# Attention outputs kept in DRAM as high and low part, and layer 1's turns in another place

## The chip, the cores and the metric

The kernel runs on one core of a Trainium2 chip. The metric is device time in microseconds (us): the median of three runs of the whole program. The engines are TensorE (PE), VectorE (DVE), ScalarE (ACT), GpSimd (POOL) and SyncE (SP); each takes its instructions from its own queue in order, and they wait for each other by semaphores.

## What is computed

Two layers of a diffusion trunk on 512 latent tokens and 256 context tokens of width 1024. Layer 0 mixes tokens by differential attention (8 heads, each with two 64-wide maps), layer 1 by neighbourhood attention on an 8 x 64 grid (16 heads of 64, taken two at a time as 8 groups). Each is followed by an output projection and a squared-ReLU MLP. Cut to what matters:

```python
for i in range(2):
    h_l = modulate(rms_norm(x, norm1_g[i]), mod_l[0], mod_l[1])      # h_c likewise, from ctx
    y = mixer_i(h_l, h_c)                   # attention, then @ w_o
    x = x + mod_l[2] * y_l
    x = x + mod_l[5] * squared_relu_mlp(modulate(rms_norm(x, norm2_g[i]), ...))
    # layer 0 updates ctx in the same way

def diff_attend(q, k, v, lam):              # layer 0
    p = softmax(einsum('bqhmd,bkhmd->bhmqk', q, k) * scale)
    return einsum('bhqk,bkhe->bqhe', p[:, :, 0] - lam * p[:, :, 1], v)
    # then rms_norm per head with gain subln_g, then @ w_o

# layer 1: a query sees an 8 x 16 window of the latent grid, with a relative bias, and all context
# y = softmax(q k + bias) v @ w_o
```

All products are fp32 made of three passes: an operand is kept as a high part (an ACT copy that rounds to the PE's fp32r form) and a low part (the value less the high part, on DVE or POOL), and `PASSES` multiplies high by high, high by low and low by high. A tile of such *parts* is `[128, 2, n]` with the part as its middle index.

## The kernel before

Per layer the kernel runs an attention stage and then its MLP. The attention stage is software-pipelined over heads (layer 0) or groups (layer 1). Inside it PE, SP and POOL issue in the order in which the program is written, and that order is a string of words (`END0`, `CYCLE1` and so on, lines 38 to 53) which `run()` goes through, once per head. DVE and ACT are placed by a scheduler from what depends on what. A word is a kind and a tile number, and a prime sends it to the head before. The kinds:

- `w`, `c`: loads of a weight chunk (SP) and its split in parts (`wsplit`, lines 145 and 146: ACT copies, POOL or, in layer 1, DVE subtracts). In the last string `c` stands for the output projection's weights.
- `Q` i, a or b: half of the QKV projection of token tile i (line 408; twelve matmuls to a half). The second half ends in a norm per head (`qk_normed`, lines 415 to 423), whose result is the tile Y.
- `U`: the *turn*: transposes of q and k of two token tiles (line 499; in layer 1 lines 634 and 636) and their splits into parts (`q_split`, `k_split`, lines 427 to 450).
- `S`: scores and softmax (lines 517 to 529; in layer 1 lines 656 to 670). `T`: probabilities transposed and split (lines 541 to 544; 686 to 688). `V`: weighted sum (line 552; 701), in layer 1 with the output put into a tile T `[128, 512]` by lines 708 and 709.
- `O` (layer 0): the normed output is transposed (line 569), and line 570 copies it on ACT into a tile OT; after every second one line 575 stores 128x256 of it, one value per element, to `oT0` in DRAM. Layer 1's fourth `V` of a group stores 128x512 to `oT1` (line 713).
- `x`: the projection's fetch of a head from `oT0` or `oT1` on SP's queue (line 738), into a staging tile N (layer 1: ST). `X`: the split of that head into parts on ACT (line 743) and then POOL or DVE (line 744), into a tile H or Q.
- `P` i, a or b: the projection of token tile i from three heads each (line 750); `B`: its last weights and gates; `m`, `n`: a chunk of the modulation vectors (lines 257 and 263).

The last head's output does not go through DRAM: `split_last` (lines 782 and 783) splits it into parts where it is made. `END0` and `END1` are the tails of the two attention stages, in which the last head's attention runs beside the projection; what is left of the projection follows in `end()`.

The table of PSUM banks gives tag A two or three banks (projections and turns), B two (T, V and O), S and C the scores and layer 0's turns. Since a bank must be read before it is written again, PE at a `T`, `V` or `O` waits for whoever reads the bank two of them back.

Of the kernel before, what the change touches and what calls it, by code (L numbers as in the profile page):

```python
# [63 lines left out]
class Block:  # L64
# [391 lines left out]
    def head0(self, h, w=None, hT=None, accs=None, split=None):  # L456
# [6 lines left out]
        def tile_(i, acc):  # L463
# [10 lines left out]
            else:  # L474
                t2 = self.sbt('OT' if accs else 'Y', [P, 2, 2, 64])
# [251 lines left out]
    def project(self, l, wo, oT, t0, xsrc, tag_o, tag_h, tag_p, out):  # L727
# [5 lines left out]
        oHL, raws, w0, x0, acc = {}, {}, [], [], {}  # L733
        gate = {}

        def fetch(h):
            st = raws[h] = self.sbt('ST' if 'ST' in self.room else 'N', [P, ntok])
            nc.sync.dma_start(st, oT[h])

        def split(h, eng):  # L740
            st = raws.pop(h)
            u = oHL[h] = self.sbt(tag_o[h // 4], [P, 2, ntok], F32R)
            self.tc.keep_in_program_order(nc.scalar.activation(u[:, 0, :], st, AF.Copy))  # L743
            self.tc.keep_in_program_order(eng.tensor_sub(u[:, 1, :], st, u[:, 0, :].bitcast(F32)))
# [33 lines left out]
        def split_last(st, j):  # L778
            if KT - 1 not in oHL:
                oHL[KT - 1] = self.sbt(tag_o[1], [P, 2, ntok], F32R)  # L780
            u, cc = oHL[KT - 1], slice(256 * j, 256 * j + st.shape[1])
            nc.scalar.activation(u[:, 0, cc], st, AF.Copy)
            nc.vector.tensor_sub(u[:, 1, cc], st, u[:, 0, cc].bitcast(F32))

        def end():
# [147 lines left out]
def hybrid_block(tc, a, out):  # L933
    nc = tc.nc
    with ExitStack() as ctx, ExitStack() as st:
# [9 lines left out]
        with b.psum_phase("ps0", **PS_HEAD0):  # L945
# [184 lines left out]
```

## Time and profile before

| | us |
|---|---|
| median of three runs | 1907.71 (1907.19 to 1908.19) |
| profiled execution | 1907.34 |
| its span on the core | 1905.4 |
| PE busy in it | 1793.9 (94%) |
| DVE, ACT, POOL busy | 1132.7, 829.2, 815.6 |
| mean granted PE clock | 0.979 |

The span is what the profiler saw between the first and the last instruction; 1.9 us of the execution lie around it. Two lines of the profile's page show the course of the span in 40 slices of 47.6 us (a digit is the busy share in tenths, 9 for 90% or more):

```profile
PE   6989999996999999999999998999998989999998
PEclk9999999997999999999999998999999999999999
```

Layer 0's attention takes the first 11 slices and ends in the tenth and eleventh, its MLP goes to the 22nd, layer 1's attention from the 25th to the 32nd, and its MLP is the rest. Stages are told by their stretch in us from the start of the span. In the views below, an operation's line number is that of the kernel before; `PA<-W,Q` names what is written and read by the program's tile names; x12 is a count. A wait is idle time of an engine before an instruction and the instruction that ended it.

### The profile page before, as it was taken

The page shows a single profiled execution, that of the slowest core. Times are in us where ns is not written, and L with a number is a line of the kernel's source. Part 1 is how long each engine was busy: PE and PEld are TensorE (multiplying, and loading weights), DVE is VectorE, ACT ScalarE, POOL GpSimd, SP SyncE. Part 2 cuts the span into 40 slices and gives each one's busy share as a digit, 9 for nine tenths or more (in the row PEclk, how much of TensorE's full clock was granted, in tenths as well). Part 3 has the DMA queues.
Part 4 walks back from the last instruction along what each step waited for, and adds up shares of the span by engine and source line. Part 5 has one row for each costly group of instructions (what it writes and reads, how often), then busy time and mean ns, then how long its engine had stood idle before and what let it go on. Part 6 is the DMA issues. An engine that isn't in the chain of part 4 may idle for free.

```text
span 1905.4 us, 27130 instructions
## 1 busy us (share of the span) xinstructions
PE 1793.9 (94%) x10256; PEld 1570.9 (82%) x10256; DVE 1132.7 (59%) x2158; ACT 829.2 (44%) x1854; POOL 815.6 (43%) x688
## 2 busy tenths in 40 slices
PE   6989999996999999999999998999998989999998
PEld 5878888885789888888888977998898778888886
DVE  4588777785574343343334676778777664444446
ACT  4476767774342212221221245677667342223321
POOL 3655656653224333342442532344335444444443
PEclk9999999997999999999999998999999999999999
DMA  8122222224324343443432132122112323223232
GB/s 327 43 84 78 87 87 87 89 69 159 119 72 140 130 157 111 166 165 112 157 136 73 56 100 64 56 69 84 56 67 89 116 89 99 89 89 107 92 100 77
DMA packets 66499, 197.61 MB, mean 104 GB/s; under 512 B 8192, under 2 KB 23488, under 8 KB 60224
## 3 DMA queue, kind: packets, MB, share of 16 engines
q1 hardware_dynamic: 58608, 186.03, 29.3%
q10 hardware_dynamic: 7760, 9.85, 1.5%
q8 instruction: 80, 1.31, 0.3%
q14 instruction: 51, 0.42, 0.1%
HBM read 180.74 MB, written 15.11 MB: 103 GB/s over the span
## 4 chain that ended last, share of the span: by engine, by line
PE 75%; DVE 11%; ACT 6%; issue 4%; POOL 2%; DMA 2%; ACTq 0%; SPq 0%; POOLq 0%; DVEq 0%
PE PD L830 22%; PE PA L408 14%; PE PA L865 11%; PE PB L865 9%; PE PA L750 4%; PE PA L257 2%; PE PS L517 2%; PE PB L552 2%; PE PB L701 2%; PE PQ L398 1%; PE PS L656 1%; PE PB L686 1%; ACT E L523 1%; PE PB L541 1%; DVE N L311 1%
## 5 line engine op out<-in xcount | busy, mean ns | idle before, releaser
L146 POOL TENSOR_TENSOR W<-R,W 128x1024 fp32r<-128x1024 f32 x142 | 351.3, 2484 | 541.2 <-ACT W L145 541.0
L830 PE MATMUL PD<-Q,W 128*128 128x384 f32 (+2 forms) x1992 | 395.9, 345 | 2.4 <-DVE Q L334 1.1
L830 PEld LDWEIGHTS PD<-Q,W 128*128 128x128 f32 x1992 | 345.7, 188 | 33.7 <-issue 8.6
L145 ACT ACTIVATE W<-R 128x1024 fp32r<-128x1024 f32 (+1 forms) x172 | 172.6, 1021 | 450.5 <-PE PA L865 193.5
L865 PE MATMUL PA<-W,H 128*128 128x512 f32 x1080 | 275.4, 393 | 4.7 <-POOL W L146 3.0
L865 PEld LDWEIGHTS PA<-W,H 128*128 128x128 f32 x1080 | 200.2, 188 | 51.5 <-issue 4.5
L839 DVE TENSOR_TENSOR N<-N 128x768 f32<-128x768 f32 (+1 forms) x64 | 67.0, 1048 | 279.1 <-ACT N L835 170.3
L865 PE MATMUL PB<-W,H 128*128 128x512 f32 x840 | 209.2, 391 | 0.0
L408 PE MATMUL PA<-W,Q 128*128 128x384 f32 (+1 forms) x1008 | 177.4, 331 | 11.2 <-ACT H L446 11.2
L865 PEld LDWEIGHTS PB<-W,H 128*128 128x128 f32 x840 | 157.4, 188 | 33.3
L408 PEld LDWEIGHTS PA<-W,Q 128*128 128x128 f32 x1008 | 163.0, 196 | 12.9 <-ACT H L446 12.9
L296 POOL TENSOR_TENSOR SQ<-SQ,half 128x4 f32<-128x4 f32 (+1 forms) x96 | 99.2, 1034 | 134.0 <-DVE SQ L421 132.9
L842 DVE SCALAR_TENSOR_TENSOR H<-N,H 128x768 fp32r<-128x768 f32 (+1 forms) x64 | 98.1, 1534 | 25.7 <-ACT H L841 25.0
L408 PE MATMUL PA<-WB,H 128*128 128x384 f32 x576 | 108.4, 340 | 0.8 <-DVE Q L469 0.8
L750 PE MATMUL PA<-W,H 128*128 128x512 f32 x384 | 99.1, 409 | 8.0 <-ACT H L743 5.1
L408 PEld LDWEIGHTS PA<-WB,H 128*128 128x128 f32 x576 | 98.6, 188 | 1.8 <-DVE Q L469 1.1
L830 PE MATMUL PD<-H,W 128*128 128x512 f32 (+1 forms) x408 | 94.1, 378 | 2.5 <-DVE SA L290 2.0
L876 DVE TENSOR_TENSOR H<-PA,H 128x512 f32<-128x512 f32 x78 | 53.9, 690 | 69.6 <-PE PA L865 69.6
L750 PEld LDWEIGHTS PA<-W,H 128*128 128x128 f32 x384 | 73.3, 196 | 26.3 <-ACT H L743 5.4
L830 PEld LDWEIGHTS PD<-H,W 128*128 128x128 f32 x408 | 73.8, 188 | 18.0 <-DVE H L334 2.9
L523 ACT ACTIVATE E<-PS,SA 128x768 f32<-128x768 f32 (+1 forms) x96 | 72.8, 759 | 34.6 <-DVE SA L522 31.9
L517 PE MATMUL PS<-Q,Q 128*128 128x256 f32 (+1 forms) x320 | 69.1, 348 | 19.4 <-ACT Q L446 10.3
(210 smaller groups left out, 3056.5 us busy)
## 6 DMA issues: line engine op xcount, KB each, us to landing
R<-in_w_dram SPq DMA_DIRECT2D x128, 512.0 KB
M<-in_wmod_dram SPq DMA_DIRECT2D x48, 1024.0 KB
R<-in_wqa_dram SPq DMA_DIRECT2D x32, 384.0 KB
R<-in_wqb_dram SPq DMA_DIRECT2D x32, 384.0 KB
Y<-in_rpb_dram SPq DMA_DIRECT2D x48, 128.0 KB
bias<-Y SPq DMA_DIRECT2D x48, 128.0 KB
X<-bias SPq DMA_DIRECT2D x8, 768.0 KB
R<-in_woa_dram SPq DMA_DIRECT2D x8, 512.0 KB
```

Of the source, the lines that this page charges most:

```text
L145: high = nc.scalar.activation(w[:, 0, :n], raw, AF.Copy)
L146: low = (eng or nc.gpsimd).tensor_sub(w[:, 1, :n], raw, w[:, 0, :n].bitcast(F32))
L296: nc.gpsimd.tensor_tensor(r, ss, self.half[:, :n], op=ALU.pow)
L408: nc.tensor.matmul(acc[:, :n], hT[kt][:, x, P * i:P * i + P], w[kt // 2][:, y, o:o + n], start=(kt == 0 and p == 0), stop=(kt == KT - 1 an ...
L517: nc.tensor.matmul(s[:, c0:c1], q[:, m, P * i:P * i + P], k[:, m, c0:c1], start=p == 0, stop=p == 1)
L523: nc.scalar.activation(e[:, m, :nk], s, AF.Exp, bias=mx[:, 0:1], accum_out=sm[:, m:m + 1])
L750: nc.tensor.matmul(ps, oHL[h][:, x, c:c + P], w[h // 2][:, y, 512 * (h % 2):512 * (h % 2) + 512], start=(first and h == hs[0] and p == 0), ...
L830: nc.tensor.matmul(ps[:, at:at + b1 - b0], w[kt // 4][:, x, o:o + P], hT[kt][:, y, b0:b1], start=(kt == 0 and p == 0), stop=(kt == KT - 1 ...
L839: nc.vector.tensor_mul(r, r, r)
L842: nc.vector.scalar_tensor_tensor(u[:, 1, :], r, 1.0, u[:, 0, :].bitcast(F32), op0=ALU.mult, op1=ALU.subtract)
L865: nc.tensor.matmul(ps, hd[:, x, P * i - c0:P * i - c0 + P], w[f][:, y, 512 * n:512 * n + 512], start=(f == 0 and p == 0), stop=(f == len(h ...
L876: nc.vector.tensor_add(av, ps, av)
```

## The change

There are four parts.

1. The DRAM tensors `oT0` and `oT1` hold both parts of each output, so that a head is twice the bytes: 768 KB for 384 in layer 0, 512 KB for 256 in layer 1.
2. The parts are made where an output is made. In layer 0's `O`, ACT writes the high part from PSUM and a new DVE operation (128x128, line 571 of the changed kernel) the low part; the store waits for both, and OT has one buffer of twice the size instead of two. In layer 1's fourth `V`, an ACT copy and a DVE subtraction 128x512 go into a new tile OS, which is stored. The last head writes straight into the projection's tile.
3. The projection's fetch goes by DMA straight into its tile of parts, and the words `X` are gone, with their ACT, POOL and DVE instructions and the staging buffers. The fetches stand elsewhere in the tails.
4. In layer 1's strings, V2'' stands right behind T3'', ahead of U4', and U2 right behind Q4b. `END1` is written anew.

The core of the diff:

```diff
-END0 = """x0 x1 x2 x3 S1' O2'' O3'' V4'' T0' U4' n1' X0 V5'' T1' X1 S2' O4'' X2 x4 V0' S3' x5 P0a O5'' T2' X3 P1a
-X4 V1' O0' S4' X5 B0 P0b m0 V2' O1' x6 P1b T3' n0 P2a T4' S5' P2b O2' P3a V3' V4' P3b m1 T5' P4a O3' n1
-X6 P4b V5' P5a P5b O4' O5'"""
-CYCLE1 = """w0 w1 Q0a T3'' U4' Q1a c0 w2 V2'' V3'' Q0b S0' Q1b Q2a S1' Q2b Q3a T0' S2' Q4a c1 w3 T1' Q3b S3' V0' U0
-Q4b Q5a c2 T2' Q5b c3 U2 V1'"""
...
-END1 = """x3 x4 T3'' c1 U4' V2'' V3'' S0' X3 x5 P2a S1' c2 X4 P3a T0' S2' X5 T1' P4a B0 S3' V0' V1' P2b T2' x6 P3b
-T3' V2' X6 P4b V3' P5a P5b"""
+END0 = """x0 x1 x2 S1' O2'' O3'' V4'' T0' U4' n1' V5'' T1' S2' O4'' x3 x4 x5 V0' S3' P0a O5'' T2' P1a V1' O0' S4'
+B0 P0b m0 V2' O1' P1b T3' n0 x6 P2a T4' S5' P2b O2' P3a V3' V4' P3b m1 T5' P4a O3' n1 P4b V5' P5a P5b O4'
+O5'"""
+CYCLE1 = """w0 w1 Q0a T3'' V2'' U4' Q1a c0 w2 V3'' Q0b S0' Q1b Q2a S1' Q2b Q3a T0' S2' Q4a c1 w3 T1' Q3b S3' V0' U0
+Q4b U2 Q5a c2 T2' Q5b c3 V1'"""
...
+END1 = """x3 x4 x5 T3'' V2'' c1 U4' V3'' S0' c2 P2a S1' P3a T0' S2' P4a T1' B0 S3' P2b V0' P3b V1' T2' x6 P4b T3'
+V2' P5a V3' P5b"""
@@ output(i), layer 0
-                oTs[j] = self.sbt('OT', [P, 256])
-            pt = self.pst('B')
+                oTs[j] = split(j) if split else self.sbt('OT', [P, 2, 256], F32R)
+            pt, o = self.pst('B'), oTs[j][:, :, at:at + P]
             nc.tensor.transpose(pt[:, :P], ons.pop(i), self.ident)
-            nc.scalar.activation(oTs[j][:, at:at + P], pt[:, :P], AF.Copy, scale=self.subg[:, 0:1])
-            if i % 2 == 1:
-                if split:
-                    split(oTs[j], j)
-                else:
-                    nc.scalar.dma_start(self.oT0[h][:, 256 * j:256 * j + 256], oTs[j])
+            nc.scalar.activation(o[:, 0], pt[:, :P], AF.Copy, scale=self.subg[:, 0:1])
+            nc.vector.scalar_tensor_tensor(o[:, 1], pt[:, :P], self.subg[:, 0:1], o[:, 0].bitcast(F32),
+                                           op0=ALU.mult, op1=ALU.subtract)
+            if i % 2 == 1 and not split:
+                nc.scalar.dma_start(self.oT0[h][:, :, 256 * j:256 * j + 256], oTs[j].bitcast(F32))
@@ weigh(u), layer 1
             if m == 1 and split:
-                split(oT[:, cols], jp)
+                o, src = split(jp), oT[:, cols]
             elif u == 3:
-                nc.scalar.dma_start(self.oT1[g], oT)
+                o, src = self.sbt('OS', [P, 2, NLAT], F32R), oT
+            else:
+                return
+            nc.scalar.activation(o[:, 0], src, AF.Copy)
+            nc.vector.tensor_sub(o[:, 1], src, o[:, 0].bitcast(F32))
+            if not split:
+                nc.scalar.dma_start(self.oT1[g], o.bitcast(F32))
@@ project
         def fetch(h):
-            st = raws[h] = self.sbt('ST' if 'ST' in self.room else 'N', [P, ntok])
-            nc.sync.dma_start(st, oT[h])
-
-        def split(h, eng):
-            st = raws.pop(h)
-            u = oHL[h] = self.sbt(tag_o[h // 4], [P, 2, ntok], F32R)
-            self.tc.keep_in_program_order(nc.scalar.activation(u[:, 0, :], st, AF.Copy))
-            self.tc.keep_in_program_order(eng.tensor_sub(u[:, 1, :], st, u[:, 0, :].bitcast(F32)))
+            oHL[h] = self.sbt(tag_o[h], [P, 2, ntok], F32R)
+            nc.sync.dma_start(oHL[h].bitcast(F32), oT[h])
...
-        def split_last(st, j):
+        def split_last(j):
             if KT - 1 not in oHL:
-                oHL[KT - 1] = self.sbt(tag_o[1], [P, 2, ntok], F32R)
-            u, cc = oHL[KT - 1], slice(256 * j, 256 * j + st.shape[1])
-            nc.scalar.activation(u[:, 0, cc], st, AF.Copy)
-            nc.vector.tensor_sub(u[:, 1, cc], st, u[:, 0, cc].bitcast(F32))
+                oHL[KT - 1] = self.sbt(tag_o[KT - 1], [P, 2, ntok], F32R)
+            return oHL[KT - 1][:, :, 256 * j:256 * j + 256]
```

`LAST1` follows `CYCLE1` in both moves. The tags of the buffers become strings with a tag per head (layer 1: three heads in H, five in Q), one temporary of layer 0's first head takes a buffer of another tag, and layer 1 opens OS with one buffer in place of ST with two. In layer 0 the order of PE is the same as before throughout. The tables below show three places where the order of an engine's instructions changes (output and inputs by tile name and number, then the shape, and how many in a row).

PE in a cycle of layer 1, from the end of Q4b to U2: before, with Q5a (first four rows of line 408 behind Q4b's last), T2' (line 686), Q5b and the first transpose of U2 (line 634),

```order
L408 MATMUL PA_12256<-W_11939,Q_6661 128x384 x3
L408 MATMUL PA_12389<-W_11563,Q_6654 128x384 x3
L408 MATMUL PA_12389<-W_11563,Q_6655 128x384 x3
L408 MATMUL PA_12389<-W_11765,Q_6656 128x384 x3
L408 MATMUL PA_12389<-W_11765,Q_6657 128x384 x3
L686 MATMUL PB_12407<-ident,E_12231 128x128 x4
L686 MATMUL PB_12414<-ident,E_12231 128x128 x4
L408 MATMUL PA_12389<-W_11898,Q_6658 128x384 x3
L408 MATMUL PA_12389<-W_11898,Q_6659 128x384 x3
L408 MATMUL PA_12389<-W_11939,Q_6660 128x384 x3
L408 MATMUL PA_12389<-W_11939,Q_6661 128x384 x3
L634 MATMUL PA_12446<-ident,Y_12192 128x128
```

and now, where U2's transposes are lines 633 and 635:

```order
L408 MATMUL PA_12280<-W_11977,Q_6679 128x384 x3
L633 MATMUL PA_12413<-ident,Y_12216 128x128
L635 MATMUL PA_12413<-ident,Y_12216 128x128
L633 MATMUL PA_12413<-ident,Y_12326 128x128
L635 MATMUL PA_12413<-ident,Y_12326 128x128
L408 MATMUL PA_12430<-W_11584,Q_6672 128x384 x3
L408 MATMUL PA_12430<-W_11584,Q_6673 128x384 x3
L408 MATMUL PA_12430<-W_11786,Q_6674 128x384 x3
L408 MATMUL PA_12430<-W_11786,Q_6675 128x384 x3
L685 MATMUL PB_12448<-ident,E_12255 128x128 x4
L685 MATMUL PB_12455<-ident,E_12255 128x128 x4
```

U2 has come ahead of Q5a, T2' and Q5b. Its transposes read the Y tiles of Q2 and Q3.

PE in the same cycle at the seam to the next one: before, T3'' (line 686), U4' (634, 636), Q1a (408) and then V2'' (701),

```order
L686 MATMUL PB_12495<-ident,E_12312 128x128 x4
L686 MATMUL PB_12502<-ident,E_12312 128x128 x4
L634 MATMUL PA_12509<-ident,Y_12379 128x128
L636 MATMUL PA_12509<-ident,Y_12379 128x128
L634 MATMUL PA_12509<-ident,Y_12433 128x128
L636 MATMUL PA_12509<-ident,Y_12433 128x128
L408 MATMUL PA_12531<-W_12040,Q_6654 128x256 x3
L408 MATMUL PA_12531<-W_12040,Q_6655 128x256 x3
L408 MATMUL PA_12531<-W_12269,Q_6656 128x256 x3
L408 MATMUL PA_12531<-W_12269,Q_6657 128x256 x3
L701 MATMUL PB_12549<-N_12405,H_11580 128x256 x4
L701 MATMUL PB_12549<-N_12406,H_11580 128x256 x2
```

and now, with T3'' as line 685, V2'' as line 700 and U4' as lines 633 and 635:

```order
L685 MATMUL PB_12519<-ident,E_12336 128x128 x4
L685 MATMUL PB_12526<-ident,E_12336 128x128 x4
L700 MATMUL PB_12533<-N_12446,H_11601 128x256 x4
L700 MATMUL PB_12533<-N_12447,H_11601 128x256 x2
L700 MATMUL PB_12533<-N_12447,H_11601 128x128 x2
L700 MATMUL PB_12533<-N_12447,VM_12056 128x128 x2
L633 MATMUL PA_12546<-ident,Y_12403 128x128
L635 MATMUL PA_12546<-ident,Y_12403 128x128
L633 MATMUL PA_12546<-ident,Y_12474 128x128
L635 MATMUL PA_12546<-ident,Y_12474 128x128
L408 MATMUL PA_12568<-W_12074,Q_6672 128x256 x3
```

V2'' (four rows, ten matmuls) has come between T3'' and U4'.

DVE at the same seam: the last step of Q5's v (line 621), the norms of Q4 and Q5 (421, 423), weight splits (146), the turn U2 (437), the output of V1' (709) and the split of T3'' (688), before,

```order
L621 TENSOR_TENSOR H_12084<-PA_12389,H_12084 128x2x64
L423 SCALAR_TENSOR_TENSOR Y_12379<-Y_12379,SQ_12384 128x256
L146 TENSOR_TENSOR W_12443<-R_12272,W_12443 128x768
L437 SCALAR_TENSOR_TENSOR H_12352<-PA_12446,gqk,H_12352 64x256
L421 TENSOR_REDUCE SQ_12436<-sq_83 128x4
L709 TENSOR_TENSOR T_12348<-PB_12463,T_12348 64x256
L437 SCALAR_TENSOR_TENSOR H_12352<-PA_12446,gqk,H_12352 64x256
L688 TENSOR_TENSOR N_12493<-PB_12495,N_12493 128x512
L423 SCALAR_TENSOR_TENSOR Y_12433<-Y_12433,SQ_12438 128x256
```

and now, with the lines of layer 1 one lower (620, 708, 687):

```order
L620 TENSOR_TENSOR H_12108<-PA_12430,H_12108 128x2x64
L421 TENSOR_REDUCE SQ_12477<-sq_83 128x4
L146 TENSOR_TENSOR W_12443<-R_12077,W_12443 128x768
L146 TENSOR_TENSOR W_12484<-R_12296,W_12484 128x768
L423 SCALAR_TENSOR_TENSOR Y_12474<-Y_12474,SQ_12479 128x256
L708 TENSOR_TENSOR T_12372<-PB_12487,T_12372 64x256
L687 TENSOR_TENSOR N_12517<-PB_12519,N_12517 128x512
L687 TENSOR_TENSOR N_12518<-PB_12526,N_12518 128x512
```

Both weight splits now stand right ahead of the output of V1', and the turn's rows are no longer between.

More of the change, by code (lines that the diff above doesn't have):

```diff
@@ L794, in end @@
                 gated(ps, xh[i, 0], i, 0, x0[(i - t0) // 3][:, (i - t0) % 3, :])
-            hT = [self.sbt(tag_h[kt // 4], [P, 2, T], F32R) for kt in range(KT)]
+            hT = [self.sbt(tag_h[kt], [P, 2, T], F32R) for kt in range(KT)]
             out.extend((xh, hT))
@@ L804, in end @@
                     self.modulated(xns, (i - 1, i), l, 1, hT, tag_p)
-        return dict(weights=weights, begin=begin, fetch=fetch, split=split, step=step, split_last=split_last, end=end)
+        return dict(weights=weights, begin=begin, fetch=fetch, step=step, split_last=split_last, end=end)
     def mlp(self, l, t0, xh, hT, tag, mid, done, side):
@@ L950, in hybrid_block @@
             b.close("M", "N")
-            b.open("right", M=1, O=4, OT=2, WB=4)
+            b.open("right", M=1, O=4, OT=1, WB=4)
             mods.load(True)
@@ L979, in hybrid_block @@
                 own = {"P": lambda n: proj["step"](2 * int(n[0]) + (n[1] == "b")), "B": lambda _: proj["begin"](),
-                       "x": lambda n: proj["fetch"](int(n)),
-                       "X": lambda n: proj["split"](int(n), (nc.gpsimd, nc.vector)[int(n) % 3 == 2])}
+                       "x": lambda n: proj["fetch"](int(n))}
                 run(END0, HEADS0, heads, load, split, **mod, **own)
@@ L1035, in hybrid_block @@
                 own = {"P": lambda n: proj["step"](2 * int(n[0]) + (n[1] == "b")), "B": lambda _: proj["begin"](),
-                       "x": lambda n: proj["fetch"](int(n)),
-                       "X": lambda n: proj["split"](int(n), nc.gpsimd)}
+                       "x": lambda n: proj["fetch"](int(n))}
                 for c in range(GROUPS1):
```

28 lines of the change are left out of this document (14 added, 14 removed).

## The prediction

> **What bounds the kernel now.** I read the share of each engine, then a table by stage, then what TensorE (PE) waits for in the stages that are not full, then the timelines of two of those places.
>
> By stage (columns: the stretch in us, its length, busy us and instructions of PE, of its weight loads, DVE, ACT and POOL, the granted clock, the DMA share, GB/s):
>
> ```profile
> 170.00:430.00 260.00, 248.35 (x1697) 227.25 (x1695) 207.01 (x493) 182.61 (x529) 153.45 (x200) 1.00 0.26 87
> 430.00:512.00 82.00, 65.17 (x323) 49.55 (x323) 51.05 (x91) 34.47 (x84) 24.56 (x17) 0.85 0.41 143
> 552.00:1050.00 498.00, 496.76 (x2817) 432.07 (x2817) 201.77 (x284) 116.72 (x154) 177.64 (x104) 1.00 0.41 135
> 1180.00:1455.00 275.00, 256.99 (x1761) 251.26 (x1759) 206.82 (x477) 192.20 (x482) 113.14 (x124) 0.96 0.21 69
> ```
>
> PE bounds the whole. Layer 0's MLP (552 to 1050) holds it 99.8% of the time at full clock, layer 1's MLP is of the same kind, and the change gives both the same matmuls in the same order, so they cost what they cost. Time can only come from the holes: 16.8 us in the end of layer 0's attention (430 to 512, END0), 18.0 in layer 1's cycles, those of layer 1's end, and the clock lost beside them (0.85 and 0.96). The 11.6 us of holes in layer 0's cycles stay, as PE's order there does.
>
> PE's waits in END0 (what it waited for: us in all, times, longest):
>
> ```profile
> PE PA L750 <- ACT H L743: 5.1, 1, 5.1
> PE PS L517 <- ACT Q L446: 4.4, 2, 2.4
> PE PS L517 <- ACT E L523: 3.3, 1, 3.3
> PE PA L750 <- DVE T L755: 2.2, 2, 1.4
> PE PA L257 <- DVE T L755: 0.8, 1, 0.8
> PE PA L750 <- DVE H L744: 0.5, 1, 0.5
> ```
>
> L743 and L744 split a fetched head into high and low part: the work that the change deletes. Layer 1's cycles:
>
> ```profile
> PE PA L408 <- ACT H L446: 9.5, 6, 1.6
> PE PA L634 <- DVE Y L423: 4.8, 6, 1.3
> PE PB L686 <- DVE T L709: 3.3, 7, 1.4
> ```
>
> These three sum to 17.6 of the 18.0 us, and all lie at one seam per cycle of 40 us: Q1a, U4' and T3'' in the text of CYCLE1. That is 2.6 us a cycle. The second half of one such seam on PE (start, us, line, count, idle before it and releaser; the last row is Q0b, of the same shape as Q1a in the third):
>
> ```profile
> 1214.02 0.33 PE L634 MATMUL PA<-ident,Y 128*128 128x128 f32 x1 [0.70 <-DVE Y L423]
> 1214.19 0.27 PE L636 MATMUL PA<-ident,Y 128*128 128x128 f32 x1
> 1216.04 2.54 PE L408 MATMUL PA<-W,Q 128*128 128x256 f32 x12 [1.59 <-ACT H L446]
> 1218.38 1.76 PE L701 MATMUL PB<-N,H 128*128 128x256 f32 x8
> ...
> 1220.20 1.10 PE L701 MATMUL PB<-N,H 128*128 128x256 f32 x8
> ...
> 1221.36 1.64 PE L408 MATMUL PA<-W,Q 128*128 128x256 f32 x12
> ```
>
> The matmuls behind the gaps run slow: 2.54 for 1.64 and 1.76 for 1.10, 1.6 us more. With the 2.6 us idle the seam loses 4.2 by these rows, some 4.8 with the small matmuls between; I use **4.8**. The clock of 0.96 over 275 us says that most of the seams, not all, are so.
>
> **END0: the split words go.** Fourteen instructions leave: seven on ACT, five on POOL, two on DVE.
>
> ```profile
> 464.03 0.83 ACT L743 ACTIVATE H<-N 128x768 fp32r<-128x768 f32 x1
> ```
>
> - P0b waits 5.1 us for the L743 that ACT comes to at 464.03, then 0.5 for the L744 behind it, and the 0.8 of L257 hangs on the same chain. Of these 6.4 I take **6.3**: the operands are whole once x5 has landed.
>
> ```profile
> 434.41 0.35 DVE L561 SCALAR_TENSOR_TENSOR O<-O,SO,one 128x128 f32<-128x128 f32 x1
> ...
> 437.79 1.72 DVE L561 SCALAR_TENSOR_TENSOR O<-O,SO,one 128x128 f32<-128x128 f32 x1
> ```
>
> ```profile
> 437.55 1.81 POOL L744 TENSOR_TENSOR H<-N,H 128x768 fp32r<-128x768 f32 x1
> ```
>
> - L561 takes 1.72 us where it starts inside the L744 of 437.55, and 0.35 without. DVE's step of the turn, for which L446 and so U4' and S2' wait, stands behind it. Of the 4.4 and 3.3 us I take back that 1.4 and one L743 (0.83) ahead of an exponential: some **2.4** with what follows.
>
> ```profile
> 448.78 3.70 PE L750 MATMUL PA<-W,H 128*128 128x512 f32 x9
> ...
> 453.35 2.33 PE L750 MATMUL PA<-W,H 128*128 128x512 f32 x9
> ```
>
> - The clock: nine equal matmuls take 3.70 and 2.33. 0.85 over 82 us is 12 us of clock lost, in stretches that follow gaps. With the longest gap and some of the rest gone I take **3** (0 to 6).
>
> Together 6.3 + 2.4 + 3 = **-12**, from -4 (P0b's waits alone, a third of them taken over by the next producer) to -16.
>
> The Trainium skill ("SBUF — State Buffer", section "SBUF: two separate sides") has VectorE with two SBUF inputs and GpSimd exclude each other on a shared pair of ports, and the 1.72 agrees. By it all of DVE's two-input work that met an L744 gets its time back, where the sum counts one.
>
> What the fetch costs instead: 768 KB each for 384.
>
> ```profile
> 424.32 15.38 SPq L738 DMA_DIRECT2D N<-oT  x6
> ```
>
> ```profile
> 426.00:432.00 6.00, 4.67 (x25) 4.27 (x25) 4.02 (x12) 3.16 (x11) 2.51 (x4) 0.72 1.01 408
> ```
>
> Six issues took 15.4 us, for 2.36 MB, with waits for free buffers between them; now they have buffers of their own. 4.72 MB at the 408 GB/s of a stretch with full queues are 11.6 us, and they are all there by 440, with the weight load ahead of them by 443; P0a starts at 448.8. Nothing, then, under cover of U4', S2' and the transposes. Without that cover, at the 153 GB/s of those 15.4 us, they end at 455: 6 us on P0a, which would make the -12 a -6. That lies inside the range above.
>
> **Layer 0's outputs.** 48 DVE operations 128x128 come in, six a head; the nearest row is L561's 0.35. The last head's six take the place of its splits. The other 42 (14.7 us of DVE) stand in cycles where DVE is busy 207 of 260 us, and two of them, of O2'' and O3'', come ahead of the turn that S2' waits for. The store waits for them on ACT's queue, 0.35 or a DVE queue's length later, with the exponentials of the next scores behind it. 0 to 0.7 for each of six cycles: **+2** (0 to +4.5). One output buffer for two: a whole run of projection matmuls lies between each store and the next write, so I cost it at nothing.
>
> **Layer 1's seam.** V2'' (the 1.10 us above) goes ahead of U4', and U2 from behind Q5b to behind Q4b. U4' and Q1a then find their operands ready: U4' comes 1.1 us later, and U2's keys are off DVE and ACT some five us sooner. So 0.70 + 1.59 go. What comes:
>
> ```profile
> 1201.22 4.46 PE L408 MATMUL PA<-W,Q 128*128 128x384 f32 x24
> ```
>
> ```profile
> 1204.41 0.82 DVE L423 SCALAR_TENSOR_TENSOR Y<-Y,SQ 128x256 f32<-128x256 f32 x1
> ...
> 1210.01 0.96 DVE L146 TENSOR_TENSOR W<-R,W 128x768 fp32r<-128x768 f32 x1
> ```
>
> - U2 now follows Q4b, the first half of these 24 matmuls, which ends near 1203.6. Its third transpose reads the Y that L423 finishes at 1205.2: 1.6 us on, less 0.25 for two transposes. **+1.0 to +1.5**, where U2 waited for nothing. Behind it on PE stand Q5a and all the rest.
> - T3'' needs the bank that DVE's L709 frees behind V1'. On DVE both weight splits of c2 and c3 (0.96 each) now come ahead of that L709, and the turn's work no longer does: some 1.3 later, **1.65** for 0.33.
> - V2'' right behind T3'' waits some **0.2** for its turned half.
> - A copy on ACT and a subtraction on DVE, 128x512, come in per group; the nearest rows for that size, 0.6 to 0.7 us, are those of the deleted splits. No wait of PE stands behind them: the store feeds a fetch a cycle later.
>
> That is 2.9 to 3.4 idle for 2.6: the idle time doesn't fall. Its crowding does. 2.3 of the 2.6 lay within 2.7 us, and slow matmuls followed; now gaps of 1.4 and 1.7 stand some 7 us apart. I give the slow stretch (1.6 to 1.7) a third of a chance: 3.2 + 0.6 = 3.8 for 4.8, **-1.0** a seam (-2 to +1), and over seven seams **-7** (-14 to +7).
>
> The Trainium skill ("TensorE: Matmul & The Clock Gate", section "Why this matters for your kernels") asks for no idle gaps over some 3 us between bursts. The rows differ: gaps of 0.70 and 1.59 are followed by matmuls at half speed. By the page no seam would be slow any more, which is the third rival.
>
> **Layer 1's end.**
>
> ```profile
> PE PB L686 <- DVE N L688: 2.1, 3, 1.2
> PE PS L656 <- ACT H L446: 1.5, 1, 1.5
> PE PB L701 <- DVE N L688: 1.3, 1, 1.3
> PE PA L750 <- POOL Q L744: 1.1, 1, 1.1
> ```
>
> L744's 1.1 goes, and POOL's splits no longer meet DVE, which should take part of L688's 3.4. S0' stands closer behind U4' (up to +0.7 on the 1.5), and c1's weights queue on SP behind x3 to x5, which wait for matmuls of Q5a. **-3** (-8 to +2).
>
> **Sum:** -12 + 2 - 7 - 3 = -20. The profiled run took 1907.34 us (span 1905.4), 0.4 under the median of 1907.71: 1887.3 from the one, 1887.7 from the other. I say **1888**.
>
> **Rivals.**
>
> 1. *Slower: the seam gets worse*, at U2 and T3''. If L423 comes as late as at its worst in the run (2.8, below), T3'' waits 2.7, and both gaps bring a slow stretch, a seam loses 5.5 + 3.4 = 8.9 for 4.8: +4.1 by seven is +29, with -13 for the rest 1924. The sign turns once a seam loses over 6.7. For it: both new waits hang on DVE, busy 207 of 275 us. Against: L423 and the splits stood where the rows show, and that bounds U2's wait by 1.5. Chance 0.11.
>
> ```profile
> PE PA L634 <- DVE Y L423: 8.4, 8, 2.8
> ```
>
> 2. *END0's holes are taken over.* V2', T3' and S5' stand behind P0b; if the softmax that feeds them sets the end and not the splits, only -4 comes: 1896. For it: the 3.3 on L523 is such a wait. Against: DVE is busy 51 of 82 us there and ACT 34. Chance 0.20.
> 3. *No slow stretch at the seams.* They lose 3.2 for 4.8, -11 in all: 1884, and 1880 with END0 at -16. Against: a gap of 1.7 is longer than the 1.59 that one followed. Chance 0.15.
> 4. *Little comes of it*: seams at +1 each and END0 at -6 give 1907.7 + 7 - 6 + 2 - 3 = 1908. Chance 0.09.
>
> The forecast's own case (1884 to 1893) has 0.45. Faster by over 0.2% (3.8 us, about what a measurement can tell from no change) holds it and rivals 2 and 3: **0.80**; within 0.2% 0.09; slower 0.11. The range, 1876 to 1904, leaves out the first rival, most of the fourth, and the far end of the third.
>
> **What would show it.** END0 some 12 us shorter, no wait of L750 for a split, its clock above 0.9. Layer 1's cycle at 39 for 40 us; U2 waiting for L423 near 1.2, T3'' for L709 near 1.7, Q1a for nothing. Layer 0's cycles 0 to 0.7 longer. Wrong would be: P0a waiting for a DMA, L634 waiting over 2 us, or a clock below 0.96 in layer 1's cycles.

## The result, and the profile after

| | us |
|---|---|
| before, median of 4 runs beside it | 1907.45 (1907.09 to 1908.19) |
| after, median of 4 runs | 1926.63 (1921.62 to 1927.59) |
| ratio after to before | 1.0095 (95% interval 1.0077 to 1.0113) |
| profiled execution after, its span | 1926.01, 1923.3 |
| PE busy in it, mean granted clock | 1797.2 (93%), 0.978 |

The change makes the kernel 0.95% slower; 20 us faster was forecast. To see where the 17.9 us of span come from, the matmuls of both traces were laid beside each other and the start of the same piece of PE's work was compared at some places:

| stretch, us of before | work | change, us | forecast |
|---|---|---|---|
| 0 to 112 | first head | +1.4 | 0 |
| 112 to 170 | START0 | +1.5 | in the +2 |
| 170 to 427 | layer 0's cycles | +0.2 | +2 |
| 427 to 531 | END0 and the rest of the projection | -0.4 | -12 |
| 531 to 1149 | layer 0's MLP | 0.0 | 0 |
| 1149 to 1186 | head of layer 1, first seam | +2.6 | -1 |
| 1186 to 1437 | six cycles of layer 1 | +5.6 | -6 |
| 1437 to 1555 | END1 and the rest of the projection | +4.3 | -3 |
| 1555 to end | layer 1's MLP | +2.7 | 0 |

The first row varies by some 2 us between runs of kernels that are the same there. The table by stage of after, END0 and layer 1's cycles (columns as in the prediction):

```profile
430.00:512.00 82.00, 63.86 (x331) 50.26 (x332) 48.61 (x100) 29.38 (x79) 15.82 (x16) 0.85 0.53 194
1180.00:1455.00 275.00, 249.80 (x1712) 244.55 (x1713) 205.90 (x471) 188.99 (x468) 108.61 (x121) 0.96 0.22 75
```

POOL's work in END0 fell from 24.56 to 15.82 us and ACT's from 34.47 to 29.38: the splits are gone. But PE is busy for less of the same stretch, and its clock is still 0.85. What PE waited for in END0 up to 490 us (us in all, times, longest):

```profile
PE PB L552 <- DVE O L556: 7.6, 1, 7.6
PE PS L517 <- ACT E L523: 4.9, 2, 3.1
...
PE PA L257 <- DVE T L754: 1.6, 1, 1.6
```

No wait for a split is left, yet one wait of 7.6 us has come. In layer 1's cycles (1186 to 1466):

```profile
PE PB L685 <- DVE T L708: 14.4, 7, 2.3
PE PA L633 <- DVE Y L423: 9.0, 6, 1.5
```

These are T3'' and U2, the two places that the prediction named. Q1a's wait, 9.5 us before, is gone, as forecast; 9.0 at U2 and 14.4 at T3'', for 3.3, have come. One seam on PE's timeline (start, us, line, count, idle before and releaser):

```profile
1210.62 0.33 PE L633 MATMUL PA<-ident,Y 128*128 128x128 f32 x1 [1.48 <-DVE Y L423]
...
1221.43 0.66 PE L685 MATMUL PB<-ident,E 128*128 128x128 f32 x4 [2.25 <-DVE T L708]
1222.15 1.70 PE L700 MATMUL PB<-N,H 128*128 128x256 f32 x8
...
1224.80 2.17 PE L408 MATMUL PA<-W,Q 128*128 128x256 f32 x12
1226.81 1.06 PE L700 MATMUL PB<-N,H 128*128 128x256 f32 x8
1227.92 1.64 PE L408 MATMUL PA<-W,Q 128*128 128x256 f32 x12
```

The gap at U2 is followed by full speed, that at T3'' by matmuls at 1.70 for 1.06 and 2.17 for 1.64. On DVE's timeline of that place T3'' waits behind two weight splits in a row, and ahead of L708 stands the norm of another projection too:

```profile
1218.35 2.03 DVE L146 TENSOR_TENSOR W<-R,W 128x768 fp32r<-128x768 f32 x2 [0.71 <-ACT W L145]
1220.30 0.61 DVE L423 SCALAR_TENSOR_TENSOR Y<-Y,SQ 128x256 f32<-128x256 f32 x1
1220.94 0.43 DVE L708 TENSOR_TENSOR T<-PB,T 64x256 f32<-64x256 f32 x1
```

In END0 the 7.6 us come from ACT's queue. Its timeline there (the idle times before an issue are shown at the instruction behind it, ended by the landing of a fetch from `oT0`):

```profile
435.70 0.36 ACTq L245 DMA_DIRECT2D C<-in_mask_dram  x1
436.11 0.47 ACT L523 ACTIVATE E<-PS,SA 128x256 f32<-128x256 f32 x1 [4.00 <-DMA H<-oT]
...
441.17 0.52 ACTq L574 DMA_DIRECT2D oT<-OT  x1
441.74 0.37 ACT L555 ACTIVATE O<-PB,SA 128x128 f32<-128x128 f32 x1 [5.06 <-DMA H<-oT]
...
445.69 0.24 ACTq L268 DMA_DIRECT2D gates<-T  x1
445.97 0.38 ACT L433 ACTIVATE Q<-PC 64x256 fp32r<-64x256 f32 x1 [3.04 <-DMA H<-oT]
```

ACT stands still for 4.00 + 5.06 + 3.04 = 12.1 us at three DMA issues that have nothing to do with the fetches. In the trace the 492 DMAs of the program signal eight semaphores, which all queues use in turn, and the instruction ahead of each of these three issues waits until the last user of its semaphore has landed. In the changed program the three (a mask load, head 6's store, a gates store) come after fetches of 768 KB that SP has just issued, and draw the semaphores of x1, x3 and x5, which land at 435.6, 441.1 and 445.6; before the change they drew those of DMAs issued 9 us or more earlier, and waited for none. The exponentials and copies behind them on ACT, and PE's weighted sum, wait with them.

### The profile page after: what moved, and what is told of

Read it like the earlier page. It is cut to its first block, busy times and chain, and to the rows that moved or that the text cites. A ratio compares the mean times of both kernels' runs of the same rounds, so it can differ in the third digit from the quotient of the medians.

```text
span 1923.3 us, 27173 instructions
## 1 busy us (share of the span) xinstructions
PE 1797.2 (93%) x10256; PEld 1573.6 (82%) x10256; DVE 1147.1 (60%) x2208; ACT 826.2 (43%) x1844; POOL 799.2 (42%) x676
## 4 chain that ended last, share of the span: by engine, by line
PE 74%; DVE 12%; ACT 6%; issue 4%; DMA 2%; POOL 2%; SPq 0%; ACTq 0%; POOLq 0%; DVEq 0%
PE PD L827 22%; PE PA L408 13%; PE PA L862 11%; PE PB L862 9%; PE PA L749 4%; PE PS L517 2%; PE PA L257 2%; PE PB L552 2%; PE PQ L398 1%; PE PS L655 1%; PE PB L685 1%; PE PB L700 1%; PE PB L541 1%; ACT E L523 1%; DMA H<-oT 1%
## 5 line engine op out<-in xcount | busy, mean ns | idle before, releaser
L827 PE MATMUL PD<-Q,W 128*128 128x384 f32 (+2 forms) x1890 | 373.6, 344 | 2.4 <-DVE Q L334 1.1
L827 PEld LDWEIGHTS PD<-Q,W 128*128 128x128 f32 x1890 | 327.7, 189 | 30.1 <-issue 8.6
L862 PE MATMUL PA<-W,H 128*128 128x512 f32 x864 | 228.3, 395 | 3.5 <-POOL W L146 1.9
L862 PEld LDWEIGHTS PA<-W,H 128*128 128x128 f32 x864 | 159.8, 188 | 41.3 <-issue 4.5
L862 PE MATMUL PB<-W,H 128*128 128x512 f32 x672 | 171.9, 392 | 0.0
L296 POOL TENSOR_TENSOR SQ<-SQ,half 128x4 f32<-128x4 f32 (+1 forms) x96 | 95.2, 992 | 138.5 <-DVE SQ L421 137.6
L862 PEld LDWEIGHTS PB<-W,H 128*128 128x128 f32 x672 | 125.9, 188 | 27.6
L827 PE MATMUL PD<-H,W 128*128 128x512 f32 (+1 forms) x510 | 118.0, 383 | 1.7 <-DVE H L334 1.7
L827 PEld LDWEIGHTS PD<-H,W 128*128 128x128 f32 x510 | 93.9, 193 | 20.7 <-DVE H L334 2.2
L749 PE MATMUL PA<-W,H 128*128 128x512 f32 x360 | 91.6, 408 | 3.1 <-DVE T L754 3.1
L522 DVE TENSOR_REDUCE SA<-PS 128x1 f32<-128x768 f32 (+1 forms) x96 | 74.5, 776 | 19.8 <-PE PS L517 10.4
L749 PEld LDWEIGHTS PA<-W,H 128*128 128x128 f32 x360 | 69.1, 196 | 19.8 <-DVE T L754 4.2
```

The source lines that it names most:

```text
L296: nc.gpsimd.tensor_tensor(r, ss, self.half[:, :n], op=ALU.pow)
L522: nc.vector.tensor_reduce(mx, s, op=ALU.max, axis=AX, negate=True)
L749: nc.tensor.matmul(ps, oHL[h][:, x, c:c + P], w[h // 2][:, y, 512 * (h % 2):512 * (h % 2) + 512], start=(first and h == hs[0] and p == 0), ...
L827: nc.tensor.matmul(ps[:, at:at + b1 - b0], w[kt // 4][:, x, o:o + P], hT[kt][:, y, b0:b1], start=(kt == 0 and p == 0), stop=(kt == KT - 1 ...
L862: nc.tensor.matmul(ps, hd[:, x, P * i - c0:P * i - c0 + P], w[f][:, y, 512 * n:512 * n + 512], start=(f == 0 and p == 0), stop=(f == len(h ...
```

## The experiments

Each kernel starts from another one of the list. They were run in three groups (e1 to e4, e5 to e8, e9 to e12), each on one chip beside the kernel before (1906.84, 1907.09 and 1907.16 us); a ratio is to before of its own group. Line numbers of the experiments shown are 5 below those of after. One table for all: median, ratio to before, and, from the profiled execution, the change against before of the stretches that matter.

| kernel | median, us (runs) | ratio, 95% interval | START0 | END0 | six cycles | END1 | MLP1 |
|---|---|---|---|---|---|---|---|
| after | 1926.63 (4) | 1.0095, 1.0077 to 1.0113 | +1.5 | -0.4 | +5.6 | +4.3 | +2.7 |
| e1_acks | 1920.40 (4) | 1.0074, 1.0059 to 1.0089 | +1.5 | -2.4 | +4.2 | +5.0 | +2.7 |
| e2_u2_back | 1903.37 (10) | 0.9985, 0.9975 to 0.9995 | +1.5 | -2.1 | -11.7 | +3.9 | +2.7 |
| e3_v2_back | 1922.81 (4) | 1.0084, 1.0069 to 1.0099 | +1.5 | -2.7 | +4.9 | +4.5 | +2.7 |
| e4_both_back | 1915.65 (7) | 1.0042, 1.0030 to 1.0054 | +1.5 | -1.7 | +0.5 | -0.5 | +2.7 |
| e5_mlp_tag | 1903.72 (10) | 0.9986, 0.9977 to 0.9995 | +1.5 | -2.2 | -11.9 | +1.9 | +3.6 |
| e6_m0_later | 1904.43 (10) | 0.9985, 0.9975 to 0.9994 | +1.5 | -4.6 | -9.2 | +7.1 | +2.7 |
| e7_end1 | 1905.66 (10) | 1.0001, 0.9988 to 1.0014 | +1.5 | -2.6 | -11.9 | +6.6 | +2.7 |
| e8_layer1_only | 1902.90 (10) | 0.9980, 0.9970 to 0.9991 | -0.2 | -1.7 | -8.9 | +7.0 | +2.7 |
| e9_hidden_h | 1901.48 (8) | 0.9973, 0.9963 to 0.9984 | +1.5 | -2.7 | -11.9 | +6.4 | 0.0 |
| e10_l0_before_h | 1901.67 (9) | 0.9971, 0.9960 to 0.9983 | -0.2 | -1.1 | -11.6 | +7.2 | 0.0 |
| e11_m0_h | 1900.99 (5) | 0.9964, 0.9951 to 0.9977 | +1.5 | -3.7 | -11.9 | +6.4 | 0.0 |
| e12_c1_h | 1902.54 (10) | 0.9976, 0.9967 to 0.9986 | +1.5 | -4.6 | -9.1 | +7.1 | 0.0 |

A single profile's stretch is good to some 2 or 3 us where clocks and DMAs vary: e2 and e6 have the same program from 531 on and differ by 2.5 in the cycles and 3.2 in END1. The 2.5 go with one seam: the sixth stays at full clock in e2 and is at half clock for 6.8 us in e6, and so it is in e8 and e12.

### ACT's stop in END0

```diff
-... S2' O4'' x3 x4 x5 V0' S3' P0a O5'' T2' P1a V1' O0' S4' B0 P0b m0 ...
+... S2' O4'' V0' S3' P0a O5'' T2' P1a V1' O0' S4' x3 x4 x5 B0 P0b m0 ...
```

> The changed kernel with x3 x4 x5 written behind S4' instead of behind O4'' in END0. SyncE's queue and its six fetches in a row stay as they are; what changes is which earlier DMA the three DMAs on ScalarE's queue wait for (the mask load, the store of head 6, the gates store): in the changed kernel each waits for one of the fetches to land, here for older ones. Theory A (ScalarE stands still behind those three waits, 12.1 us in all, and the V5'' that waits 7.6 us stands still with it): the hole of 7.6 us goes, END0 is 7 to 9 us shorter than in the changed kernel, time 1917 to 1919. Rival B (the fetches of 4.7 MB take the DMA bandwidth, whatever waits for them): no difference, 1924 to 1927.

The 7.6 us wait is gone and ACT no longer stands behind a fetch. The fetches did not stay in a row, as was expected: x4 and x5 now wait for the semaphores of x0 and x1 themselves and go out at 432.6 and 434.5. So this run alone does not part the semaphores from the load of six fetches at once; the landings above do. END0 is 2.0 us shorter than in after, not 7.6. What took the rest, on PE's timeline and on DVE's (L749 here is after's L754, the gating of P0a):

```profile
446.79 2.92 PE L512 MATMUL PS<-Q,Q 128*128 128x512 f32 x8 [3.15 <-ACT E L518]
...
465.42 1.94 PE L252 MATMUL PA<-M,silu 128*32 128x256 f32 x16 [4.21 <-DVE T L749]
```

```profile
461.22 0.96 DVE L517 TENSOR_REDUCE SA<-PS 128x1 f32<-128x768 f32 x1 [0.80 <-ACT E L518]
...
463.75 1.02 DVE L524 SCALAR_TENSOR_TENSOR E<-E,SA 128x768 f32<-128x768 f32 x1
464.68 0.68 DVE L749 TENSOR_TENSOR T<-PA,N 128x512 f32<-128x512 f32 x1
```

The first wait is for the softmax of the scores before, as before the change (3.3). In the second, new one, the gating stands behind S4's softmax in DVE's queue. Before, P0b waited 5.1 us for a split; now m0, the next word, waits 4.2 for this. In after, where the 7.6 us come first, it waits 1.6.

### U2 or V2''

Layer 1's two moves were undone apart, each on top of e1.

```diff
 e2_u2_back (CYCLE1; LAST1 in the same way)
-... Q4b U2 Q5a c2 T2' Q5b c3 V1'
+... Q4b Q5a c2 T2' Q5b c3 U2 V1'
 e3_v2_back (CYCLE1; LAST1 and END1 in the same way)
-... T3'' V2'' U4' Q1a c0 w2 V3'' ...
+... T3'' U4' Q1a c0 w2 V2'' V3'' ...
 e4_both_back: both
```

> e1_acks with U2 put back behind Q5b and c3 in layer 1 (CYCLE1, LAST1); V2'' stays right behind T3''. Theory U (U2 is what hurts: it waits 1.5 us a cycle for the norm of Q3, and it lets both weight splits stand ahead of the operation that frees T3'''s bank, 2.1 us): both waits go, 8 us less than e1_acks, and as V2'' covers part of Q1a's wait of before a further 3 to 9: 1901 to 1908. Rival V (V2'' ahead of U4' is what hurts, since it puts U4' and S0' later): no better than e1_acks, 1916 to 1920.

> e1_acks with V2'' put back behind U4' and Q1a in layer 1 (CYCLE1, LAST1, END1); U2 stays behind Q4b. Theory U: U2's 1.5 and T3'''s 2.1 us stay and nothing is won, 1917 to 1922. Rival V: the seam gets as short as before or shorter, 1908 to 1913.

> e1_acks with both U2 and V2'' back, so that layer 1's cycles have the order of before and only the parts kept in DRAM are left. Theory U and V alike: cycles of 40.0 us as before, 8 us less than e1_acks, 1909 to 1911. If it is 1917 or more, the new ScalarE and VectorE operations of the store cost the cycles their time, not the order.

U2's move is what hurts: taking it back is worth 15.9 us of the six cycles (+4.2 to -11.7) and 17.0 of the median, and the kernel is then faster than before. V2''s move alone gains 12 (e2 against e4, 1903.37 and 1915.65). With U2 early it gains nothing that the runs tell (e1 against e3), and U2's move costs 7 without it (e3 against e4) for the 17 with it. e4 was expected at 1909 to 1911, with the cycles of before. Its profiled run, 1911.23, has them (+0.5) and is among the fastest of its seven; what the others lose, no profile shows. T3'' comes round every 38.2 us in e2 and every 40.1 before. Its PE timeline at the place shown above:

```profile
1213.27 0.66 PE L680 MATMUL PB<-ident,E 128*128 128x128 f32 x4 [0.32 <-DVE T L703]
1214.52 1.15 PE L695 MATMUL PB<-N,H 128*128 128x256 f32 x8 [0.59 <-DVE N L682]
...
1217.32 1.70 PE L403 MATMUL PA<-W,Q 128*128 128x256 f32 x12 [0.96 <-ACT H L441]
```

Idle are 0.32, 0.59 and 0.96, 1.9 in all, and the matmuls behind run at full speed. DVE comes to T3'''s read (L703 here) soon after one weight split, with no second one:

```profile
1210.84 0.96 DVE L141 TENSOR_TENSOR W<-R,W 128x768 fp32r<-128x768 f32 x1
...
1212.79 0.43 DVE L703 TENSOR_TENSOR T<-PB,T 64x256 f32<-64x256 f32 x1
```

In after, ACT is busy with U2's keys when the weight copies of c2 and c3 come up, does both in a row (1.56 us), and DVE their subtractions in a row, ahead of the read. The clock at the six seams, in windows of 8 us (length, PE busy and count, granted clock, DMA share, GB/s): first of before, then of after, then of e2:

```profile
1213.00:1221.00 8.00, 5.71 (x34) 0.79 0.04 16
...
1293.00:1301.00 8.00, 5.38 (x43) 1.00 0.13 46
...
1413.00:1421.00 8.00, 5.00 (x28) 0.81 0.01 2
```

```profile
1219.00:1227.00 8.00, 5.68 (x34) 0.79 0.33 100
...
1342.00:1350.00 8.00, 5.68 (x47) 1.00 0.31 101
```

```profile
1212.00:1220.00 8.00, 6.13 (x50) 1.00 0.18 52
...
1401.00:1409.00 8.00, 5.54 (x45) 1.00 0.49 192
```

Before and after have five slow seams of six each (the rows left out are at 0.79), e2 none (all at 1.00). The after kernel kept the slow stretch and got more idle; e2 lost both.

### Layer 1's MLP

The change also moved tiles: the second hidden tile of layer 1's MLP lies in Q, where before both lay in H. The matmul order is the same and PE never waits there, yet it takes 2.7 us longer. The first idea was that alternating tiles cost it.

```diff
-b.mlp(1, 2, xh1, hT3, 'QHQ', ...)      # e2
+b.mlp(1, 2, xh1, hT3, 'HQQ', ...)      # e5: both hidden tiles in Q
```

> e2_u2_back (1903.4 us) with the tags of layer 1's MLP set to H, Q, Q for Q, H, Q: its accumulators in H tiles and both hidden tiles of a chunk in Q tiles, where the changed kernel has one in H and one in Q. In every run of the changed kernel's family the MLP of layer 1 is 3.05 us longer than before though PE waits for nothing in it. Theory M (matmuls whose stationary operand comes alternately from an H and a Q tile issue 5 ns apart more): the MLP takes 3.0 us less, 1900 to 1901. Rival N (it comes from the activations, three of which stand in Q and five in H, for four and four): no difference in the MLP, 1903.

That fell: +3.6. The time from one such matmul's start to the next, worked out from the trace, was 227.2 ns before (626 pairs, stationary operand in H), 232.5 in e5 (631 pairs, in Q) and 230 to 234 in the mixed kernels. e5 moved the accumulators too, from Q to H. So all hidden tiles were put back in H and the accumulators left in Q, with the head's and the norm's tiles exchanged for it:

```diff
-b.project(1, ..., 'HHHQQQQQ', 'QQQHHHHH', 'S1', done)    b.mlp(1, ..., 'QHQ', ...)
+b.project(1, ..., 'HHHQQQQH', 'QQQQHHHH', 'S1', done)    b.mlp(1, ..., 'QHH', ...)
```

> The kernel of e2_u2_back, with layer 1's tiles placed so that both hidden tiles of its MLP lie in H, as before the change ('HHHQQQQH', 'QQQQHHHH', 'QHH'). Theory Q (matmuls whose stationary operand is a hidden tile in Q are issued 232 ns apart, in H 227 ns): MLP1 from 1555 to its end loses its +2.7 and is within 0.7 us of before's, the spacing there is 227 ns; about -2.7 against e2's kernel: ratio about 0.997. Rival (the MLP's 2.7 come with the clock or the run, not with the tiles): MLP1 stays over +2 and the spacing at 230 or more.

MLP1 is exactly as before, 0.0, at 227.2 ns again. The groups of PE's instructions in layer 1's MLP show it (shape, count, busy, mean ns, idle before), first of after, then of e9:

```profile
L862 PE MATMUL PA<-W,Q 128*128 128x512 f32 x162 | 46.5, 395 | 0.0
...
L862 PE MATMUL PB<-W,H 128*128 128x512 f32 x162 | 46.2, 393 | 0.0
```

```profile
L857 PE MATMUL PA<-W,H 128*128 128x512 f32 x336 | 85.6, 390 | 0.0
L857 PE MATMUL PB<-W,H 128*128 128x512 f32 x331 | 84.1, 389 | 0.0
```

Why Q's place costs 5 ns a matmul stays open.

### What is left of END0

```diff
-... B0 P0b m0 V2' O1' P1b ...      # e2
+... B0 P0b V2' O1' m0 P1b ...      # e6; e11 is e9 with the same
```

> e2_u2_back with m0 behind V2' and O1' in END0. In e1_acks PE waits 4.2 us at m0 for a PSUM bank that VectorE's L749 frees, and L749 stands behind the softmax of S4' in VectorE's queue. Theory S (with the splits gone that softmax sets the end, and PE has V2' to do meanwhile): the wait falls under 2 us, END0 2 to 3 us shorter, 1900 to 1902. Rival (V2' and O1' are no sooner ready, or the wait moves to P1b): 1903 to 1904.

> e9 with m0 behind V2' O1' in END0 (e6's edit). If e6's gain of some 2.5 us in END0 is real, END0 ends some 2 us earlier against before than in e9 and the ratio is about 0.001 lower than e9's; if it was spread between runs, the same as e9's.

In the profiles END0 is 2.5 and 1.0 us shorter than in e2 and e9. m0 waits 2.7 us for 4.2, but the projection's waits on the same gating rise from 3.1 to 3.8 in all. The medians do not tell the pairs apart (1904.43 and 1903.37; 1900.99 and 1901.48). e11 has the lowest ratio of all, 0.9964 (0.9951 to 0.9977): 0.36% faster than before, though not told apart from e9 and e10.

### Layer 0 as before

e8 is e2 with all of layer 0 as before: one value per element in DRAM, staged fetches, `X` words, two OT buffers. e10 is the same on e9.

> Layer 0 as in the kernel before (one value per element in DRAM, splits X in END0), layer 1 as in e2_u2_back. Theory L (VectorE's new operation holds a PSUM bank at each O: 4.5 us of PE waits on it up to 170 us, for 1.6 on ScalarE before): up to 170 us it runs 2.5 to 3.5 us sooner than e2_u2_back, in END0 it gives 3 back: 1903 to 1905 in all. Rival (the first 170 us differ from run to run for another reason, such as the clock): no difference at 170 us, and 1905 to 1907 in all, as END0's gain is lost.

> The kernel of e8_layer1_only (layer 0 as before the change, layer 1's turns as in e2_u2_back) with e9's placing of tiles. If layer 0's part of the change is worth nothing or less, at or below e9's kernel: ratio 0.996 to 0.997, about 1900 to 1901. If it is worth its some 2 us of END0, above e9's by 1 to 3.

The ratios are the same with and without layer 0's part (0.9980 and 0.9985; 0.9971 and 0.9973). It gains nothing that these runs can tell. START0 loses 1.7 us by it in each profile. What PE waited for there (85 to 170 us), in after and then in before:

```profile
PE PB L541 <- DVE OT L571: 3.4, 2, 1.8
```

```profile
PE PB L541 <- ACT OT L570: 1.6, 2, 1.3
```

L571 is the new low part. It reads the PSUM bank behind ACT's copy, so the bank comes free later, and PE's next transposes wait for it.

### Layer 1's end

In after S0' waits 3.78 us for the keys of U4', 1.5 before, and later the gating:

```profile
1473.86 0.83 PE L655 MATMUL PS<-H,H 128*128 128x256 f32 x2 [3.78 <-ACT H L446]
...
1517.18 2.93 PE L749 MATMUL PA<-W,Q 128*128 128x512 f32 x6 [2.85 <-DVE T L754]
```

Two orders were tried against the first of these, by filling it and by clearing ACT ahead of it:

```diff
-... c1 U4' V3'' S0' c2 P2a S1' ...          # e2
+... c1 U4' V3'' P2a S0' c2 S1' ...          # e7
-... T3'' V2'' c1 U4' V3'' S0' ...           # e11
+... T3'' V2'' U4' c1 V3'' S0' ...           # e12
```

> e2_u2_back with P2a ahead of S0' in END1. S0' waits 4.0 us there for the keys that U4' makes, where before it waited 1.5. Theory T (the new END1 leaves only V3'' between U4' and S0'; 2.3 us of matmuls ahead of S0' cover that much of the wait): 2 us less, 1901 to 1902. Rival (P2a waits for its weights c1 in turn): 1903 to 1904.

> e11 with c1 behind U4' in END1, so that ACT makes U4''s keys ahead of the weight copy of c1. If S0''s wait of 3.8 us in the end of layer 1 comes from the two copies ahead on ACT, it falls to some 2 and END1 is 1 to 2 us shorter than in e11. Rival (P2a then waits for c1's parts as it did in e7): END1 the same or up to 3 longer, with a wait on L743 to L749's first matmul for W.

Neither helped. In e7 S0' no longer waits for the keys, but the projection that took its place waits 1.5 us for its weights. END1's +6.6 lies within what the other order gave (+1.9 in e5 to +7.2 in e10), and the median is 1.9 us above e5's. In e12 S0' waits 5.4 us instead of the 4.0 of e11. DVE there, then PE:

```profile
1452.70 2.16 DVE L711 TENSOR_TENSOR OS<-T,OS 128x512 fp32r<-128x512 f32 x1
1454.89 0.42 DVE L440 TENSOR_TENSOR H<-PA,H 64x256 fp32r<-64x256 f32 x1
```

```profile
1455.77 1.03 PE L650 MATMUL PS<-H,H 128*128 128x256 f32 x2 [5.40 <-ACT H L441]
```

L711 is the new low part of group 6's output, of which the prediction said "No wait of PE stands behind them". Here the keys' subtraction, which S0' needs, stands behind it in DVE's queue. It takes 2.16 us for 0.74 in e11, and S0' waits the same 1.4 longer. It starts while POOL runs its split of c1 (1451.97 to 1454.32), which the edit moved there; in e11 that split was over before.

Whether c1's copies on ACT cause the wait was not tested: DVE and ACT go by the scheduler, and ACT's order is the same in both kernels, with both copies ahead of U4''s keys (the second ends at 1444.3 in e11 and 1448.4 in e12). Before the change one such copy (1.06 us) ran, over 2 us ahead of U4'; in after two in a row (2.0 us) run while U4' is transposed. In e11 the output's split itself holds the keys up by 0.2 us at most: their high part, which the subtraction needs, ends at 1449.15, and the subtraction starts at 1449.34. So the most of S0''s wait stays open.

The gating's 2.85 in after ends with an L754 ahead of which DVE ran two operations beside POOL's weight splits: L716 took 1.80 us and L755 2.83, for 0.42 and 0.68 at other places of that trace (the last section shows L755). Before the change PE did not wait for the gating in END1. No kernel without that meeting was run, so why END1 gives back 2 to 7 us stays partly open.

## Why the prediction was wrong

The forecast was 1888 in a range of 1876 to 1904; it came out slower. The first rival (the seam gets worse at U2 and T3'') has nearly the number, 1924, but by luck: it puts +29 on the seams and -13 on the rest, and measured are +8 and some +10.

- **Layer 1's seam, -7: wrong, +8** (2.6 + 5.6). In the six cycles Q1a and U4' found their operands ready, V2'' waited for nothing, and U2's wait was 1.5, the upper bound. At the first seam, where there is no V2'' yet, U4' waited 4.0 us, for 2.8 before the change. Two steps failed. T3'' was put at 1.65, "both weight splits of c2 and c3 now come ahead of that L709": it was 2.25 or 2.26 in all six seams of the stretch. The 0.61 more is what the norm's L423 took, which stands between those splits and L708 in the table of DVE's new order ahead of the prediction, and was left out of the sum. And "I give the slow stretch a third of a chance": it came at five seams of six, as often as before. The idle per seam was 1.5 + 2.26 = 3.8 for the 2.6 before, and that covers the +0.9 a cycle (5.6 by six). The 4.8 that a seam was said to lose before was some 0.5 too high: 2.6 idle and 3.41 us at half clock make 4.3. The sum of both moves also hid what they do apart: V2'' alone gains 2 us a cycle (e2 against e4), and U2 takes more than that away (e1 against e2).
- **END0, -12: wrong, -0.4.** P0b's waits on splits went, as said. "Nothing, then" for the fetch was true of P0a, which waited for no DMA, and false of ACT, which was not looked at: its issues stopped for 12.1 us behind the fetches. With that mended (e1) only 2 came. The step "of these 6.4 I take 6.3" left out the gating of P0a, queued on DVE behind S4's softmax: the second rival, "END0's holes are taken over". The clock's 3 never came, since the gaps did not go.
- **Layer 0's outputs, +2: right in sum** (+1.7), wrong in place. The cycles lost 0.2. START0 lost 1.5, by the PSUM bank that the new DVE operation holds, a wait that the prediction counted only on the turn and the store.
- **Layer 1's end, -3: wrong, +4.3.** L744's 1.1 went. S0's wait was bounded by "up to +0.7 on the 1.5" and was 3.78. The gating, which made PE wait for nothing there before, is not in the sum at all, and made it wait 2.85 and 0.78.
- **The MLPs, "they cost what they cost": wrong for layer 1's, +2.7.** Same matmuls in the same order, but one hidden tile in another place.

Of the first rival, T3'''s wait brought its slow stretch (2.26 for the 2.7 feared) and U2's did not; the second was right that other waits take over, though less than its -4 came. What weighed against the first, "L423 and the splits stood where the rows show", took the rows of before for the new order; a scheduler places DVE and ACT anew for each order of PE. The range does not leave out the third rival's far end, as was said: that is 1880.

## What to carry to other kernels

Where two moves are made in one order, price and time each alone, and then together: here V2'' was worth 12 us alone, and U2 cost 7 alone and 17 on top of it. Moving a step earlier on PE moves its work earlier on ACT and DVE as well, so ask which reads of full PSUM banks then stand behind it. A transfer's cost is not only its bytes: look at what shares its completion semaphore, and at the queue of the engine that issues next.

## What the runs showed of the hardware

- **The clock fell after gaps of 2.3 us and less, and where they lay in time counted.** 2.25 us of idle was followed by clock 0.79 over 8 us at five seams of six, and so were the two gaps of before (0.70 and 1.59, within 2.7 us); gaps of 0.32, 0.59 and 0.96 within 5 us were followed by 1.00 at the five seams of e2 that have them. One seam with 2.26 idle stayed at 1.00, so the gap alone does not decide. In the traces the clock falls to 0.50 for 3.41 us or a multiple of it, and within a profile the falls start a whole number of 3.41 us apart (1222.50, 1263.46, 1304.42, 1386.34 and 1427.30 in after). Here are pieces of that grid in after, at the first seam and at the one that stayed fast (columns as above):

```profile
1219.09:1222.50 3.41, 1.09 (x8) 1.00 0.54 144
1222.50:1225.91 3.41, 3.41 (x19) 0.50 0.22 87
1341.97:1345.38 3.41, 1.65 (x15) 1.00 0.14 26
1345.38:1348.79 3.41, 2.85 (x23) 1.00 0.59 212
```

PE was idle for 2.32 us of the first piece; the gap of the other seam is cut by the end of a piece, with 1.76 in the third. In the layer 1 cycles of all the profiles the 27 falls follow pieces with 1.59 us or more of idle time, and every piece with 1.95 or more has a fall behind it; between the two it went both ways. The Trainium skill ("TensorE: Matmul & The Clock Gate", section "Why this matters for your kernels") asks for no gaps over some 3 us; here shorter ones were enough.
- **A matmul's pace went with where its stationary tile lay**: 227.2 ns from H, 232.5 from Q, with the same shapes and no waits.
- **A DVE addition 128x512 took 2.83 us beside a POOL split, for 0.69.** The rows are of END1: of after, DVE's and then POOL's, and of before the same addition while POOL does nothing:

```profile
1513.70 2.83 DVE L755 TENSOR_TENSOR Q<-Q,T 128x512 f32<-128x512 f32 x1
```

```profile
1511.11 4.87 POOL L146 TENSOR_TENSOR W<-R,W 128x1024 fp32r<-128x1024 f32 x2 [2.94 <-ACT W L145]
```

```profile
1497.25 0.69 DVE L756 TENSOR_TENSOR Q<-Q,T 128x512 f32<-128x512 f32 x1
```
